# Attention, second half: the key low parts as full-array products in even column tiles, from a zero-padded copy of the queries' high parts

## The chip, the cores and the metric

The kernel runs on one core of one Trainium2 chip. The metric is device time in microseconds (us): before the change 2640.49 us, the median of three runs (2640.45 to 2641.33). The profile and the trace are of one further execution, taken by the hardware profiler.

## The reference, cut to what matters

One layer of a hybrid encoder: a projection of 2048 tokens (a grid of 32 rows by 64 columns) feeds a gated linear recurrence and a 2-D neighbourhood attention with 16 heads of 64 dimensions. Both results go through one output projection. The change touches the scores of the attention alone.

```python
h = layernorm(x) * (1 + scale) + shift
proj = h @ w_in                                   # (2048, 9216)
q_h, i_h, zf_fw, zf_bw, g_h, q_n, k_n, v_n, g_n = split(proj)
y_hg = hgrn2_branch(q_h, i_h, zf_fw, zf_bw, g_h, ...)
# attention: a query at (row, col) sees a window of 8 rows x 16 columns
s = einsum('bhjqd,bhrjcd->bhjqrc', q_row, k_blk) * 64 ** -0.5
s = where(col_mask, s + bias, -inf)
o = einsum('bhjqrc,bhrjcd->bhjqd', softmax(s), v_blk)
y = concat([y_hg, o * silu(g_n)]) @ w_out
x = layernorm(alpha * x + gate * y) * ln_g + ln_b
```

## The kernel before, in words

The stages in time, in us of the profiled execution: the start (to 15), the first half of the attention (to 520), the recurrence (to 1757), the second half of the attention (to about 2320), and the rest of the output projection and the last norm (to 2639). The 16 heads are eight pairs in each half; a pair's two heads lie on partitions 0 to 63 and 64 to 127.

Products are made nearly exact with a split into a high and a low part of a shorter float type. The dense projections (L278) are three products: high x high, high x low, low x high. In the scores the same is done in two steps. Each head has a tile `Q` of 128 rows, its 64 high rows and its 64 low rows, and `KA` (for one head) or `KB` (for the other) holds the high part of the keys twice, so one product over 128 rows (L1015) gives (high + low) q x high k. The second product (L1018) adds high q x low k, with `KL` holding both heads' low parts on their halves of the partitions: 64 rows for each head, so the two heads' products use the two halves of the array.

In the second half a pair has three row blocks R = 1, 2, 3 and in each four column tiles j = 0 to 3; a tile has 128 queries per head and 360 (j = 0, 3) or 480 (j = 1, 2) keys for R = 1 and 2, and 288 or 384 for R = 3. The *even* tiles are j = 0 and 2. A tile's chain: scores on TensorE (PE) into two banks; `shifted` on VectorE (DVE, L1027) adds the bias and finds the extreme; `powers` on ScalarE (ACT, L1032) takes the exponential and its sum; `shares` on DVE (L1036, L1037) divides; `turned` transposes on PE (L1060) and copies the result to `pt`, the first head on DVE (L1064), the second on ACT (L1066); `sums` multiplies by V on PE (L1082, 64 columns of the array per head). After four tiles the output is gated on DVE into `yv` (L1092) and written to `yq` (L1093).

`natten_woven` sets PE's order by hand: scores of tile i; behind an odd tile the sums of two tiles; a piece of dense work for the next pair (L278, in the first pair also the V projection L291, in the last the output projection L1448 to L1450); the transposes of tile i−1; dense work again; then the preparation of later tiles (`st.k` L952 to L954, `st.q` L936 to L939, `st.gate` L970, `st.v` L963). So an even tile's scores are followed on PE by dense work, an odd tile's by sums. ACT, DVE, POOL and SP (which issues the DMAs) are put in order by a scheduler that estimates when things are ready; `tc.high_priority` moves work ahead in it. Weights come from DRAM to `wr`, ACT copies the high part `wh` (L778), DVE takes the rest `wl` (L779). The output projection's weights are loaded by `wo_load` and split by `wo_split` (L1408, L1409) in the last pairs. L297 copies a bank of the V projection to `vt`.

The `pbuf` tiles hold the scores from `shifted` to `turned`, used in turn; there are five in this half.

```python
if i % 2 and len(pipe) > 2:
    for _ in range(2):
        m, r, c, pts = pipe.pop(0)
        m.sums(r, c, pts)
yield 1
turn(pipe, 2)
yield 1
```

Of the kernel before, what the change touches and what calls it, by code (L numbers as in the profile page):

```python
# [10 lines left out]
F32 = mybir.dt.float32  # L11
F32R = mybir.dt.float32r
U32 = mybir.dt.uint32
AF = mybir.ActivationFunctionType
# [5 lines left out]
P = 128  # L20
# [10 lines left out]
PRI = 1500  # L31
# [7 lines left out]
def body(ctx: ExitStack, tc: tile.TileContext, t):  # L39
    nc = tc.nc  # L40
    dve, act, pool, pe = nc.vector, nc.scalar, nc.gpsimd, nc.tensor
# [85 lines left out]
    def pinned(ins):  # L127
        return tc.keep_in_program_order(ins)
# [604 lines left out]
    pbuf, pb_i = [], [0]  # L733

    def natten_init(n, half):
        pbuf.clear()
        cur["bias"] = (11, 15)[half]
        for i in range(n):
            b = tl("pbuf")
            pool.memset(b[:, 264:512], 0.0)  # L740
            pbuf.append(b)
        keysets.clear()
        for i in range(2 - half):
            keysets.append({z: tl(f"{z}{i}", F32R, [P, (12, 28)[half] * GW]) for z in ("KA", "KB", "KL")})

    NCOL = (("q", 5120), ("k", 6144), ("g", 8192))
    NCOL0 = (("k", 6144), ("q", 5120), ("g", 8192))
# [162 lines left out]
    keysets = []  # L910
# [82 lines left out]
    class Natten:  # L993
# [8 lines left out]
        def scores(self, R, j):  # L1002
            k0, nr = TILE[R]
            bt = self.st.table(KIND[R], j)
            kw = KW[j]
            nk, b0 = nr * kw, KC[j] - KS[j]
            scs = [ps("sc"), ps("sc")]
            qs = [z[:, j * P:(j + 1) * P] for z in self.st.Q[R]]
            keys = keysets[self.p % len(keysets)]

            def kv(z):
                return keys[z].rearrange("p (r c) -> p r c", c=GW)[:, k0 - self.r_base:k0 - self.r_base + nr, KC[j]:KC[j] + kw]

            for hh in range(2):
                pe.matmul(scs[hh][:, 0:nk], qs[hh], kv(("KA", "KB")[hh]), start=True, stop=False, skip_group_check=True)  # L1015
            for hh in range(2):
                hs_ = slice(hh * 64, hh * 64 + 64)
                pe.matmul(scs[hh][:, 0:nk], qs[hh][hs_], kv("KL")[hs_], start=False, stop=True, skip_group_check=True)  # L1018
            out, mxs = [], []

            def shifted(hh):
                s, sc = pbuf[pb_i[0] % len(pbuf)], scs[hh]
                pb_i[0] += 1
                mx = cp.tile([P, 3], F32, tag="mx", name=nm("mx"), bufs=6)
                out.append(s)
                mxs.append(mx)
                return dve.tensor_tensor_reduce(s[:, 0:nk].rearrange("p (r c) -> p r c", c=kw), sc[:, 0:nk].rearrange("p (r c) -> p r c", c=kw),  # L1027
                                                bt[:, 0:nr, hh, b0:b0 + kw], scale=-0.125, scalar=3.0e38, op0=ALU.add, op1=ALU.min, accum_out=mx[:, 0:1])

            def powers(hh):  # L1030
                s, mx = out[hh], mxs[hh]
                act.activation(s[:, 0:nk], s[:, 0:nk], AF.Exp, scale=-1.0, bias=mx[:, 0:1], accum_out=mx[:, 1:2])  # L1032

            def shares(hh):
                s, mx = out[hh], mxs[hh]
                dve.reciprocal(mx[:, 2:3], mx[:, 1:2])  # L1036
                dve.tensor_scalar(s[:, 0:nk], s[:, 0:nk], mx[:, 2:3], 1.0, op0=ALU.mult, op1=ALU.mult)  # L1037

            with tc.high_priority(offset=PRI):
                if self.half:  # L1040
                    for hh in range(2):
                        shifted(hh)
                        powers(hh)
                        shares(hh)
                else:
                    for hh in range(2):
                        pinned(shifted(hh))
                    for f in (powers, shares):
                        for hh in range(2):
                            f(hh)  # L1050
            return out
# [56 lines left out]
    def natten_woven(st, nxt, pipe, extra=None, finish=False):  # L1108

        n = Natten(st)  # L1110
        if st.half:
            now, later = prep_now(st), prep_next(nxt) if nxt else {}
        else:
            now, later = {0: [(st.table, "top", 3)]}, first_next(nxt) if nxt else {}
        extra = extra or {}
        for i, (R, j) in enumerate(n.order):
            pipe.append([n, R, j, n.scores(R, j)])
            if i % 2 and len(pipe) > 2:
                for _ in range(2):
                    m, r, c, pts = pipe.pop(0)  # L1120
# [4 lines that stand above are left out]
            for f, *a in now.get(i, []) + later.get(i, []) + extra.get(i, []):  # L1125
                f(*a)
        if finish:
# [3 lines that stand above are left out]
            turn(pipe, 1)  # L1131
# [13 lines left out]
    HB = {"c": 3, "qi0": 1, "qi1": 2, "v": 2, "pm": 1, "ub": 1, "Sf": 5, "Sb": 5, "pd": 1, "dec": 4, "decb": 1, "dsuf": 1, "g": 3, "ei": 1, "de": 2, "ke": 1, "kx": 1, "qx": 1, "x": 4, "t": 2, "cl": 3, "rh": 1, "rl": 1}  # L1145
    SB_ = {"ada": 4, "x": 16, "nb": 1}
    NB0 = {"V": 6, "pbuf": 4, "pt": 4, "yv": 1, "bias": 3, "x": 8, "s": 3}
    NB1 = {"V": 6, "pbuf": 5, "pt": 4, "yv": 1, "bias": 3, "Q": 6}
    SMS = {"raw": "e", "s": "sg", "w0": "bk", "w1": "q", "w2": "vt", "w2l": "gt", "vo": "vt"}
    SM0 = {"raw": "e", "Q": "q", "sg": "sg", "e": "e", "q": "q", "vo": "vt", "gt": "gt"}  # L1150
    SMH = {"V0": "gt", "e": "e", "q": "q", "vo": "vt", "gt": "gt", "sg": "sg", "raw": "e", "bk": "bk"}
    SM1 = {"raw": "e", "sg": "sg", "vo": "vt", "bk": "bk", "V2": "q", "wr": "vt", "wr2": "gt"}

    def startup():

# [203 lines left out]
    with psum_phase("n0", NPS), tc.manual_schedule(engines={mybir.EngineType.PE}):  # L1359
        with phase("st", SB_, SMS), tc.manual_schedule(engines={getattr(mybir.EngineType, e) for e in ("PE", "SP", "Activation", "DVE")}):  # L1360
            raws, feed = startup()
        with phase("n0", NB0, SM0):
            natten_init(4, 0)
            st = first_half(raws, feed)
# [146 lines left out]
    LU = 6  # L1511
    LP = 0
    with psum_phase("n1", NPS), phase("n1", NB1, SM1), tc.manual_schedule(engines={mybir.EngineType.PE}):
        natten_init(5, 1)
        st = st0
        for f, *a in ((st.k, 0), (st.k, 1), (st.k, 2), (st.q, 1), (st.table, "mid", 0), (st.table, "mid", 1), (st.v, 2), (st.v, 3), (st.table, "mid", 3), (st.q, 2), (st.v, 4), (st.gate, 1)):
            f(*a)
        vs = vstream(2, 3)
        for _ in range(5):
# [5 lines left out]
        for u in range(8):  # L1525
            nxt, extra = None, None
            if u < 7:
# [4 lines left out]
                nxt = Prep(u + 1, 1, raws)  # L1532
# [8 lines left out]
            st = nxt  # L1541
# [77 lines left out]
```

## Time and profile before

| | us |
|---|---|
| median of three runs | 2640.49 |
| lowest and highest | 2640.45, 2641.33 |
| the profiled execution's own time | 2641.48 |
| its span in the trace | 2639.3 |
| PE busy | 2574.2 (98%) |
| weight loads (PEld) busy | 2140.4 (81%) |
| DVE busy | 1738.7 (66%) |
| ACT busy | 1402.7 (53%) |
| POOL busy | 106.4 (4%) |

Lines such as L1018 are lines of the kernel before. A row of the timeline is the start, the duration of the whole row in us, the engine, line, operation, output and inputs, the tile used of the array (128*128, or 64*128 for half of its rows), the shape and the number of instructions put together in the row; behind it in brackets the idle time of the engine just before and what ended it. PE's matmuls are pipelined, so the distance of two starts says more than a duration. PEld is the load of weights into the array. A row of waits is the line that waits, what it waits for, the total, the number and the longest; "issue" stands where the trace shows nothing that the engine waited for.

### The profile page before, as it was taken

The page shows a single profiled execution, that of the slowest core. Times are in us where ns is not written, and L with a number is a line of the kernel's source. Part 1 is how long each engine was busy: PE and PEld are TensorE (multiplying, and loading weights), DVE is VectorE, ACT ScalarE, POOL GpSimd, SP SyncE. Part 2 cuts the span into 40 slices and gives each one's busy share as a digit, 9 for nine tenths or more (in the row PEclk, how much of TensorE's full clock was granted, in tenths as well). Part 3 has the DMA queues.
Part 4 walks back from the last instruction along what each step waited for, and adds up shares of the span by engine and source line. Part 5 has one row for each costly group of instructions (what it writes and reads, how often), then busy time and mean ns, then how long its engine had stood idle before and what let it go on. Part 6 is the DMA issues. An engine that isn't in the chain of part 4 may idle for free.

```text
span 2639.3 us, 45745 instructions
## 1 busy us (share of the span) xinstructions
PE 2574.2 (98%) x17140; PEld 2140.4 (81%) x17140; DVE 1738.7 (66%) x4354; ACT 1402.7 (53%) x2808; POOL 106.4 (4%) x142
## 2 busy tenths in 40 slices
PE   6999999989999999999999999999999999999998
PEld 5888888878888888888888888888777777788887
DVE  7444545477777778877787777555777778548443
ACT  4534445366666666666666666454666667431110
POOL 0000000000000000000000000000000000042221
PEclk9999999999999999999999999999999999999999
DMA  7465454212121126212221222345454455443331
GB/s 271 140 212 142 127 169 155 95 49 69 65 65 57 65 73 219 85 46 76 76 65 57 73 72 75 109 129 157 125 137 137 140 142 162 117 155 128 96 96 56
DMA packets 225629, 295.86 MB, mean 112 GB/s; under 512 B 28807, under 2 KB 117511, under 8 KB 224263
## 3 DMA queue, kind: packets, MB, share of 16 engines
q1 hardware_dynamic: 225407, 292.93, 36.3%
q8 instruction: 135, 2.21, 0.4%
q14 instruction: 87, 0.71, 0.1%
HBM read 217.65 MB, written 66.99 MB: 108 GB/s over the span
## 4 chain that ended last, share of the span: by engine, by line
PE 74%; ACT 2%; DVE 1%; DMA 1%; issue 0%; DVEq 0%; ACTq 0%
PE pj L278 40%; PE ps L1448 4%; PE ps L1450 4%; PE ps L1449 4%; PE ps L1082 3%; PE ps L1060 3%; PE pj L291 3%; PE ps L478 2%; PE ps L470 1%; PE ps L1018 1%; PE ps L1015 1%; PE ps L545 1%; PE ps L569 1%; PE ps L517 1%; PE ps L571 1%; DMA yq<-t 1%
## 5 line engine op out<-in xcount | busy, mean ns | idle before, releaser
L278 PE MATMUL pj<-h,wh 128*128 128x512 f32 x4000 | 1277.8, 400 | 4.2 <-ACT wh L803 1.9
L278 PEld LDWEIGHTS pj<-h,wh 128*128 128x128 f32 x4000 | 722.9, 188 | 163.0 <-issue 20.3
L278 PE MATMUL pj<-h,wl 128*128 128x512 f32 x2000 | 784.0, 392 | 0.0
L278 PEld LDWEIGHTS pj<-h,wl 128*128 128x128 f32 x2000 | 375.7, 188 | 83.3 <-DVE wl L779 0.4
L1032 ACT ACTIVATE pbuf<-pbuf,mx 128x480 f32<-128x480 f32 (+5 forms) x256 | 152.7, 598 | 150.1 <-DVE mx L1027 149.5
L1027 DVE CUSTOM_DVE_ANT_1 pbuf<-ps,bias 128x480 f32<-128x480 f32 (+5 forms) x256 | 129.4, 540 | 120.4 <-PE ps L1018 105.5
L291 PE MATMUL pj<-wh,h 128*128 128x256 f32 x1024 | 197.8, 288 | 2.8 <-ACT vt L297 2.5
L291 PEld LDWEIGHTS pj<-wh,h 128*128 128x128 f32 x1024 | 164.5, 193 | 7.2 <-ACT vt L297 3.2
L268 ACT ACTIVATE wh<-wr 128x512 fp32r<-128x512 f32 x192 | 120.3, 627 | 80.9 <-PE pj L278 71.8
L269 DVE TENSOR_TENSOR wl<-wr,wh 128x512 fp32r<-128x512 f32 x192 | 131.5, 685 | 45.2 <-ACT wh L268 43.7
L291 PE MATMUL pj<-wl,h 128*128 128x256 f32 x512 | 145.4, 284 | 0.0
L1066 ACT ACTIVATE pt<-ps 120x384 f32<-120x384 f32 (+3 forms) x128 | 65.3, 511 | 127.3 <-PE ps L1060 126.9
L464 DVE TENSOR_TENSOR de<-e,de 128x512 f32<-128x512 f32 x64 | 44.3, 692 | 118.0 <-ACT de L463 118.0
L1064 DVE COPY pt<-ps 120x384 f32<-120x384 f32 (+3 forms) x128 | 75.0, 586 | 68.1 <-PE ps L1060 67.4
L1060 PE MATMUL ps<-ident,pbuf 128*128 128x128 f32 (+2 forms) x832 | 112.3, 273 | 0.7 <-DVE pbuf L1037 0.7
L1060 PEld LDWEIGHTS ps<-ident,pbuf 128*128 128x128 f32 (+2 forms) x832 | 97.5, 137 | 17.1 <-ACT pbuf L1032 1.1
L752 ACT ACTIVATE e<-pj 128x512 f32<-128x512 f32 x98 | 58.4, 596 | 87.2 <-PE pj L278 80.4
L1037 DVE TENSOR_SCALAR pbuf<-pbuf,mx 128x480 f32<-128x480 f32 (+5 forms) x256 | 101.4, 408 | 4.4
L1424 ACT ACTIVATE yh<-yr 128x512 fp32r<-128x512 f32 x52 | 32.7, 629 | 131.8 <-PE ps L1449 113.5
L1497 DVE TENSOR_TENSOR vt<-ps,gt 128x512 f32<-128x512 f32 x24 | 16.5, 692 | 128.9 <-PE ps L1450 128.9
L291 PEld LDWEIGHTS pj<-wl,h 128*128 128x128 f32 x512 | 98.8, 193 | 1.5 <-issue 0.5
L445 DVE TENSOR_TENSOR_SCAN c<-c,g 128x128 f32<-128x128 f32 x256 | 88.3, 403 | 10.7 <-ACT c L435 10.7
(268 smaller groups left out, 4642.5 us busy)
## 6 DMA issues: line engine op xcount, KB each, us to landing
wr<-in_w_in SPq DMA_DIRECT2D x276, 256.0 KB
yr<-yq SPq DMA_DIRECT2D x64, 256.0 KB
bias<-tint SPq DMA_DIRECT2D x24, 480.0 KB
x<-in_x SPq DMA_DIRECT2D x32, 256.0 KB
ada<-in_ada_m SPq DMA_DIRECT2D x8, 1024.0 KB
wr<-in_w_v SPq DMA_DIRECT2D x32, 256.0 KB
nv<-vt SPq DMA_DIRECT2D x32, 256.0 KB
yq<-yv SPq DMA_DIRECT2D x32, 256.0 KB
```

The lines of the kernel that those rows point to most:

```text
L268: act.activation(hi, raw, AF.Copy)
L269: dve.tensor_tensor(lo, raw, hi, op=ALU.subtract)
L278: pe.matmul(pz, a, b, start=(k == 0 and n == 0), stop=(k == KT - 1 and n == 2))
L291: pe.matmul(pzs[tp][:, i * 256:(i + 1) * 256], a, b, start=(k == 0 and n == 0 and i == 0), stop=(k == KT - 1 and n == 2), skip_group_check ...
L445: dve.tensor_tensor_scan(c[:, sl], c[:, sl], L[:, sl], 0.0, op0=ALU.add, op1=ALU.subtract)
L1027: return dve.tensor_tensor_reduce(s[:, 0:nk].rearrange("p (r c) -> p r c", c=kw), sc[:, 0:nk].rearrange("p (r c) -> p r c", c=kw), bt[:, 0 ...
L1032: act.activation(s[:, 0:nk], s[:, 0:nk], AF.Exp, scale=-1.0, bias=mx[:, 0:1], accum_out=mx[:, 1:2])
L1037: dve.tensor_scalar(s[:, 0:nk], s[:, 0:nk], mx[:, 2:3], 1.0, op0=ALU.mult, op1=ALU.mult)
L1060: pe.transpose(ptp[0:cw, c * P:(c + 1) * P], s[:, c * cw:(c + 1) * cw], ident)
L1448: pe.matmul(pz, yh[:, kk], wh, start=first, stop=False)
L1449: pe.matmul(pz, yh[:, kk], wl, start=False, stop=False)
L1450: pe.matmul(pz, yl[:, kk], wh, start=False, stop=last)
```

## The change

In the second half a new tile `Z` of 128 rows and 2 x 512 columns (4 KB per partition) holds the high part of the queries of one row block: the first 512 columns have the first head's on rows 0 to 63 and zeros below, the second 512 the second head's on rows 64 to 127 and zeros above. POOL writes the zeros once. `alone` copies the two high parts into it on ACT, with high priority: once at the start of the half, and then behind the scores of each tile j = 2 for the next row block, or for the next pair's first one, 24 times in all. In even tiles the low product of each head is now one product over all 128 rows, `Z`'s columns against `KL`; odd tiles keep the 64-row form. To find the space, there are four `pbuf` tiles in place of five, and `yv` has no buffer of its own but takes one of the four of the tag `vt`, which the V projection's outputs and the loaded w_out weights use as well.

```diff
@@ natten_init
+        if half:
+            keysets[0]["Z"] = tl("Z", F32R, [P, 2 * 512])
+            pool.memset(keysets[0]["Z"][64:128, 0:512].bitcast(F32), 0.0)
+            pool.memset(keysets[0]["Z"][0:64, 512:1024].bitcast(F32), 0.0)
+    def alone(st, R):
+        z = keysets[0]["Z"]
+        with tc.high_priority(offset=PRI):
+            for hh in range(2):
+                hs_ = slice(hh * 64, hh * 64 + 64)
+                act.activation(z[hs_, hh * 512:(hh + 1) * 512], st.Q[R][hh][hs_], AF.Copy)
@@ scores
             for hh in range(2):
                 hs_ = slice(hh * 64, hh * 64 + 64)
-                pe.matmul(scs[hh][:, 0:nk], qs[hh][hs_], kv("KL")[hs_], start=False, stop=True, skip_group_check=True)
+                if self.half and j % 2 == 0:
+                    o = hh * 512 + j * P
+                    pe.matmul(scs[hh][:, 0:nk], keys["Z"][:, o:o + P], kv("KL"), start=False, stop=True, skip_group_check=True)
+                else:
+                    pe.matmul(scs[hh][:, 0:nk], qs[hh][hs_], kv("KL")[hs_], start=False, stop=True, skip_group_check=True)
@@ natten_woven
             pipe.append([n, R, j, n.scores(R, j)])
+            if st.half and j == 2 and (R < 3 or nxt):
+                alone(*((st, R + 1) if R < 3 else (nxt, 1)))
@@ buffers of the second half
-    NB1 = {"V": 6, "pbuf": 5, "pt": 4, "yv": 1, "bias": 3, "Q": 6}
+    NB1 = {"V": 6, "pbuf": 4, "pt": 4, "bias": 3, "Q": 6}
-    SM1 = {"raw": "e", "sg": "sg", "vo": "vt", "bk": "bk", "V2": "q", "wr": "vt", "wr2": "gt"}
+    SM1 = {"raw": "e", "sg": "sg", "vo": "vt", "yv": "vt", "bk": "bk", "V2": "q", "wr": "vt", "wr2": "gt"}
@@ start of the second half
-        natten_init(5, 1)
+        natten_init(4, 1)
-        for f, *a in (..., (st.q, 1), (st.table, "mid", 0), ...):
+        for f, *a in (..., (st.q, 1), (alone, st, 1), (st.table, "mid", 0), ...):
```

On PE no instruction changes its place. The orders of ACT and DVE do change; lines move by 12 to 16 in the changed kernel (L297 stays, the exponential L1032 is L1048, L1027 is L1043, L1037 is L1053, the copies into Z are L756). The first place is ACT at the start of the second half, before: `Q` is the high part of the queries, `sg` a gate, `vt` the V projection's output.

```order
L937 ACTIVATE Q_19061<-e_18010 64x512
L970 ACTIVATE sg_19066<-e_18260 128x512
L970 ACTIVATE sg_19348<-e_18304 128x512
L297 ACTIVATE vt_18842<-pj_18744 128x512
L297 ACTIVATE vt_18845<-pj_18745 128x512
L338 ACTIVATE sg_18714<-sg_18714 128x512
```

And the same place of the changed kernel.

```order
L949 ACTIVATE Q_19064<-e_18010 64x512
L982 ACTIVATE sg_19069<-e_18260 128x512
L982 ACTIVATE sg_19353<-e_18304 128x512
L756 ACTIVATE Z_18661<-Q_18682 64x512
L756 ACTIVATE Z_18661<-Q_18683 64x512
L297 ACTIVATE vt_18845<-pj_18747 128x512
L297 ACTIVATE vt_18848<-pj_18748 128x512
L338 ACTIVATE sg_18717<-sg_18717 128x512
```

The two copies stand ahead of the L297 that empties the V projection's banks.

The second place is ACT at tile (R = 3, j = 2) of pair 3, before: the exponentials of the two heads (`pbuf`), two weight splits (`wh`), the second head's transposed copy (`pt`), the next keys (`KA`).

```order
L752 ACTIVATE e_22140<-pj_22015 128x512
L1032 ACTIVATE pbuf_18652,mx_22152<-pbuf_18652,mx_22152 128x384
L1032 ACTIVATE pbuf_18654,mx_22157<-pbuf_18654,mx_22157 128x384
L778 ACTIVATE wh_22168<-wr_22011 128x512
L778 ACTIVATE wh_22172<-wr_22013 128x512
L1066 ACTIVATE pt_22186<-ps_22182 128x384
L952 ACTIVATE KA_3548_18660<-e_21874 64x256
```

And in the changed kernel.

```order
L764 ACTIVATE e_22165<-pj_22040 128x512
L756 ACTIVATE Z_18661<-Q_21834 64x512
L756 ACTIVATE Z_18661<-Q_21835 64x512
L790 ACTIVATE wh_22195<-wr_22036 128x512
L790 ACTIVATE wh_22199<-wr_22038 128x512
L1048 ACTIVATE pbuf_18650,mx_22177<-pbuf_18650,mx_22177 128x384
L1048 ACTIVATE pbuf_18652,mx_22182<-pbuf_18652,mx_22182 128x384
L1082 ACTIVATE pt_22213<-ps_22209 128x384
L964 ACTIVATE KA_3547_18658<-e_21897 64x256
```

Both copies and both splits now stand ahead of the exponentials; on DVE the splits' remainders (L779, now L791) accordingly stand ahead of the two shares.

The third place is DVE one tile later, before: reciprocals, shares (TENSOR_SCALAR) of tile (R = 3, j = 3) of width 288, and the shift (ISA) of the next pair's first tile, 360 wide.

```order
L1036 RECIPROCAL mx_22212<-mx_22212 128x1
L1064 COPY pt_22245<-ps_22241 128x384
L1036 RECIPROCAL mx_22217<-mx_22217 128x1
L1037 TENSOR_SCALAR pbuf_18656<-pbuf_18656,mx_22212 128x288
L1027 ISA pbuf_18650,mx_22272<-ps_22266,bias_22081 128x360
L1027 ISA mx_22272 128x1
L1037 TENSOR_SCALAR pbuf_18658<-pbuf_18658,mx_22217 128x288
L1027 ISA pbuf_18652,mx_22277<-ps_22267,bias_22081 128x360
L1027 ISA mx_22277 128x1
```

And in the changed kernel.

```order
L1052 RECIPROCAL mx_22239<-mx_22239 128x1
L1080 COPY pt_22272<-ps_22268 128x384
L1052 RECIPROCAL mx_22244<-mx_22244 128x1
L1053 TENSOR_SCALAR pbuf_18654<-pbuf_18654,mx_22239 128x288
L1043 ISA pbuf_18650,mx_22299<-ps_22293,bias_22106 128x360
L1043 ISA mx_22299 128x1
L1043 ISA pbuf_18652,mx_22304<-ps_22294,bias_22106 128x360
L1043 ISA mx_22304 128x1
L1053 TENSOR_SCALAR pbuf_18656<-pbuf_18656,mx_22244 128x288
```

The second head's share, which its transposes on PE read, now stands behind both shifts of the next pair's first tile.

More of the change, by code (lines that the diff above doesn't have):

```diff
@@ L1513, in body @@
     with psum_phase("n1", NPS), phase("n1", NB1, SM1), tc.manual_schedule(engines={mybir.EngineType.PE}):
-        natten_init(5, 1)
+        natten_init(4, 1)
         st = st0
-        for f, *a in ((st.k, 0), (st.k, 1), (st.k, 2), (st.q, 1), (st.table, "mid", 0), (st.table, "mid", 1), (st.v, 2), (st.v, 3), (st.table, "mid", 3), (st.q, 2), (st.v, 4), (st.gate, 1)):
+        for f, *a in ((st.k, 0), (st.k, 1), (st.k, 2), (st.q, 1), (alone, st, 1), (st.table, "mid", 0), (st.table, "mid", 1), (st.v, 2), (st.v, 3), (st.table, "mid", 3), (st.q, 2), (st.v, 4), (st.gate, 1)):
             f(*a)
```

## The prediction

> **What bounds the kernel now.** I read the page first, then busy time by stretch, the waits of TensorE and of its weight loads in the second half, and last the timeline of single tiles. The first fence holds the page's row of engines and the row of busy time over pairs 1 to 5 of the second half (stretch and length in us, then busy us and instructions of PE, PEld, DVE, ACT and POOL, then the TensorE clock, DMA share and GB/s).
>
> ```profile
> PE 2574.2 (98%) x17140; PEld 2140.4 (81%) x17140; DVE 1738.7 (66%) x4354; ACT 1402.7 (53%) x2808; POOL 106.4 (4%) x142
> 1858.00:2237.00 379.00, 378.32 (x2597) 298.23 (x2596) 295.97 (x896) 251.33 (x592) 5.49 (x18) 1.00 0.50 140
> ```
>
> PE is busy 378.3 of 379 us at full clock: there TensorE is the bound and nearly any time taken from its stream comes off the end. DVE (296) and ACT (251) have room on average, but what counts is where one wait ends last. The next rows are waits between 1700 and 2330 us (waiting line, what it waits for, us in total, times, longest).
>
> ```profile
> PE pj L1448 <- ACT yh L1440: 7.3, 2, 6.1
> PE pj L291 <- ACT vt L297: 2.5, 1, 2.5
> PE ps L1060 <- DVE pbuf L1037: 0.7, 1, 0.7
> PEld ps L1018 <- issue: 25.0, 96, 0.4
> ```
>
> Matmuls wait for other engines in few places, and I come back to three. The last row is where the change bites: all 96 tiles show the weight load of the half-array product (L1018) held up with nothing visible to wait for, 0.26 us each. What that costs on PE is seen in one even tile of 360 keys (start, duration, engine, line).
>
> ```profile
> 2006.27 0.32 PE L1015 MATMUL ps<-KA,Q 128*128 128x360 f32 x1
> 2006.43 0.33 PE L1015 MATMUL ps<-KB,Q 128*128 128x360 f32 x1
> 2006.69 0.43 PE L1018 MATMUL ps<-KL,Q 64*128 64x360 f32 x2
> 2007.05 0.73 PE L278 MATMUL pj<-h,wh 128*128 128x512 f32 x2
> 2007.62 0.40 PE L278 MATMUL pj<-h,wl 128*128 128x512 f32 x1
> 2007.86 0.62 PE L278 MATMUL pj<-h,wh 128*128 128x512 f32 x2
> 2008.32 0.40 PE L278 MATMUL pj<-h,wl 128*128 128x512 f32 x1
> ```
>
> Full-array products follow each other by 0.16 us (KA to KB), and projections by 0.23 (2007.62 to 2008.32 is three steps). But KB to the half-array pair takes 0.26, and the pair to the first projection 0.36, although the pair streams its 360 columns side by side (two matmuls in one row, 0.43 from the first start to the last end). The first two projections then take 0.57 where 0.46 would do. A tile of 480 keys shows the same.
>
> ```profile
> 2016.78 0.38 PE L1015 MATMUL ps<-KA,Q 128*128 128x480 f32 x1
> 2017.00 0.38 PE L1015 MATMUL ps<-KB,Q 128*128 128x480 f32 x1
> 2017.31 0.49 PE L1018 MATMUL ps<-KL,Q 64*128 64x480 f32 x2
> 2017.73 0.73 PE L278 MATMUL pj<-h,wh 128*128 128x512 f32 x2
> 2018.31 0.39 PE L278 MATMUL pj<-h,wl 128*128 128x512 f32 x1
> ```
>
> I read this as the array emptying when its row split changes, once going into the half-array form and once coming out.
>
> **The change part by part.** *The even tile.* In the new form the two low products are full-array with the same width as KA and KB, so I expect KA, KB, Z, Z, projection in even steps. With 360 keys the way from KB to the third projection now is 2007.62 − 2006.43 = 1.19; then three steps of 0.16 and two of 0.23 make 0.94: a gain of 0.25. With 480 keys it is 1.31 against 3 × 0.22 + 0.46 = 1.12: a gain of 0.19, since the added stream is longer. The six even tiles of a pair are 2 × 360, 2 × 480, 384 and 288 wide, mean 392; on the line through both points that is 0.234, and 48 tiles give **−11.2 us**. Odd tiles keep the old form.
>
> The Trainium skill, *TensorEngine Tiling (Array Packing)*, under Key Properties, says that a change of tiling mode drains the TensorE. The trace agrees as far as it shows 0.26 and 0.36 us where neighbours take 0.16 and 0.23.
>
> *What it adds.* 24 times two ACT copies of 64x512 (same form as L937 below, 0.65 a piece with its step), 31 us of ACT in 560. Two memsets on POOL are hidden: POOL is 4% busy, and they need only the space of the phase before. Four pbuf instead of five cost nothing: tile i+2 takes the buffers of tile i, whose transposes stand ahead of its scores on PE. Now the places where the copies stand ahead of somebody.
>
> *Start of the half.* The rows are ACT's queue, the PE wait, and the clock (after length and PE busy, the granted share, then DMA share and GB/s).
>
> ```profile
> 1758.04 0.63 ACT L937 ACTIVATE Q<-e 64x512 fp32r<-64x512 f32 x1
> 1758.69 1.15 ACT L970 ACTIVATE sg<-e 128x512 f32<-128x512 f32 x2
> 1759.74 1.07 ACT L297 ACTIVATE vt<-pj 128x512 f32<-128x512 f32 x2
> 1760.37 0.38 PE L291 MATMUL pj<-wh,h 128*128 128x256 f32 x1 [2.49 <-ACT vt L297]
> 1761.00:1762.00 1.00, 1.00 (x9) 0.87 0.51 112
> 1762.00:1763.00 1.00, 1.00 (x6) 0.50 0.53 143
> 1765.00:1766.00 1.00, 1.00 (x7) 0.92 0.28 83
> ```
>
> ACT goes from one to the next without a gap, and PE stands 2.49 us until L297 empties its bank. The two copies now stand ahead of L297, behind the L970s: 2 × 0.65 = **+1.3 us**, all on the path. The stall is already followed by a stretch at half clock: a share of 0.87 puts its start 0.26 us before 1762 and one of 0.92 its end 0.16 after 1765, 3.4 us in all, which cost PE half of that, 1.7. I put nothing more on it; a second such stretch, another 1.7, is the upper end, and nothing beyond 1.3 saved or lost is the lower.
>
> The Trainium skill, *TensorE: Matmul & The Clock Gate*, Part 1, describes a clock gate that judges activity in windows of some 3.4 us. By it a longer idle could spoil one more window, and the sum would be about −4.8 in place of −6.5; the low stretch here fits one window, and no run here yet shows two.
>
> *(R3, j2) in pairs 1 to 5.* Here the copies and two weight splits go ahead of both exponentials, so the chain behind them is late. Pair 3:
>
> ```profile
> 2038.87 0.56 DVE L1027 CUSTOM_DVE_ANT_1 pbuf<-ps,bias 128x384 f32<-128x384 f32 x1 [1.89 <-PE ps L1018]
> 2039.47 0.62 ACT L1032 ACTIVATE pbuf<-pbuf,mx 128x384 f32<-128x384 f32 x1 [1.41 <-DVE mx L1027]
> 2040.69 1.14 ACT L778 ACTIVATE wh<-wr 128x512 fp32r<-128x512 f32 x2
> 2041.73 0.47 ACT L1066 ACTIVATE pt<-ps 128x384 f32<-128x384 f32 x1
> 2042.63 0.94 ACT L952 ACTIVATE KA<-e 64x256 fp32r<-64x256 f32 x2 [0.43 <-PE ps L1015]
> 2043.18 0.46 DVE L1027 CUSTOM_DVE_ANT_1 pbuf<-ps,bias 128x288 f32<-128x288 f32 x1 [0.22 <-issue]
> 2048.80 0.37 DVE L1037 TENSOR_SCALAR pbuf<-pbuf,mx 128x288 f32<-128x288 f32 x1
> 2049.08 0.53 DVE L1027 CUSTOM_DVE_ANT_1 pbuf<-ps,bias 128x360 f32<-128x360 f32 x1
> 2049.55 0.82 PE L1060 MATMUL ps<-ident,pbuf 128*96 128x128 f32 x6
> ```
>
> ACT idles 1.41 us there, but the copies may only start when the product is done, at about 2038.9, where DVE starts. Then 1.3 of copies, 1.1 of splits and 1.2 of exponentials (2039.47 to 2040.69) end at 2042.5, and the shares on DVE, 0.4 each and some 0.1 for the reciprocals, at 2043.4. So L1027 of the next tile begins there at about 2043.5 in place of 2043.18, 0.3 to 0.5 later with its reading, and DVE then runs almost without a break to the L1037 at 2048.80. That share, the second head's, now ends at 2049.17; in the new order it stands behind the second L1027 of the tile after (2049.08), another 0.45 later. Its head's transposes are the second three of the row at 2049.55, needed from 2049.85 on; that leaves 0.7 today. With 0.3 + 0.45 of delay, and PE arriving up to 0.46 earlier through two even tiles just before, PE would wait 0.5: **+2.5 us** in five pairs (0.5 to 4.0, by 0.1 to 0.8 a pair).
>
> *The other j2 tiles* have the copies in the same gap, with more room behind. (R2, j2) of pair 3:
>
> ```profile
> 2021.14 0.58 ACT L1066 ACTIVATE pt<-ps 128x512 f32<-128x512 f32 x1
> 2022.96 0.83 PE L1082 MATMUL ps<-pt,V 128*64 128x128 f32 x12
> ```
>
> The copy L1066 ends at 2021.72 and its product starts 1.2 us later. Since 0.68 of the 1.3 fits into ACT's wait for DVE, I put 0.6 on L1066 and 0.2 on PE's side; it still holds with some 0.4 to spare. I take 0, at most 0.2 in each of 16 places.
>
> *Pair 6* has the weight work of the output projection as well.
>
> ```profile
> 2207.43 0.70 ACT L1032 ACTIVATE pbuf<-pbuf,mx 128x480 f32<-128x480 f32 x1 [0.68 <-DVE mx L1027]
> 2219.40 0.84 PE L1060 MATMUL ps<-ident,pbuf 128*120 128x128 f32 x6 [0.68 <-DVE pbuf L1037]
> ```
>
> From the first row to 2217 ACT has hardly a gap, and at the second PE already stands 0.68. Of the copies' 1.3, 0.68 fits into the wait of the first row; the other 0.6 is handed through ACT and DVE to the transposes, and what the tile in front gains there is lost to the wait: **+0.7 us** (0.4 to 1.5).
>
> *Pair 7.* The 6.1-us wait of L1448 is set by ACT's yh, not by PE's own pace, so the gain of the tile inside it is void: **+0.2**.
>
> *The shared buffers.* The first four w_out loads now come out of the tag that yv uses too, so the last of them waits, on SP's queue with the V loads behind it, until the yq write of pair 6's first yv.
>
> ```profile
> 2203.65 0.41 SPq L1093 DMA_DIRECT2D yq<-yv  x1
> 2213.78 1.15 ACT L1408 ACTIVATE wo<-vt 128x512 fp32r<-128x512 f32 x2
> ```
>
> From that write's issue to the split that needs the last load are 10 us, for a write and a read of 256 KB: 0, at most 1.
>
> **Sum:** −11.2 + 1.3 + 2.5 + 0.7 + 0.2 = **−6.5 us**. On the profiled execution's 2641.48 that makes 2635.0. That execution is 0.99 over the median of the three runs, with the same stages, so the forecast against the median is 2640.49 − 6.5 = **2634.0**.
>
> **The rivals.** *A, the forecast* (chance 0.55): 2634.0, give or take 1.8 for the terms' bounds.
>
> *B, all copies hidden but those at the start* (0.16). Gaps such as the 1.41 above take up the rest, and only the start's 1.3 remains: −11.2 + 1.3 = −9.9, 2630.6. For it: one wait for L1037 in the whole half today. Against it: the 0.7 us at (R3, j3), less than the delays that I count there.
>
> *C, the copies cost at nearly all 24 places* (0.2). They have priority and stand ahead of exponentials and of L1066, and a faster PE meets them sooner. At 0.3 us in each of the 18 places beside the start and (R3, j2) of pairs 1 to 5: −11.2 + 1.3 + 2.5 + 5.4 = −2.0, 2638.5. From 0.41 a place on the gain is gone. For it: ACT at 66% in these pairs (251 of 379), and slack of 0.4 to 0.7 in the tiles above. Against it: most copies fall into a wait for DVE.
>
> *D, the other side: the delay is not the switch of form* (0.09). If the 0.26 and 0.36 belonged to the low product as such (its operands, its load), they would stay, and the full-array form only adds: two products that ran side by side now go one behind the other. That is one more stream per tile, 0.16 at 360 and 0.22 at 480, 0.18 at the mean: +8.6 in 48 tiles, with the 1.3 + 2.5 + 0.7 above +13.1, 2653.6. It decides as soon as less than 0.18 of the tile's 0.41 beyond even steps (0.234 + 0.18) is due to the switch. Against it: KA to KB uses operands of the same kind at the same clock and takes 0.16, and the delay sits on both sides of the pair, also on the projections that share nothing with it. For it: no row shows this product in another form. The Trainium skill, *TensorEngine Tiling (Array Packing)*, Theoretical Speedup, gives row tiling up to 2x where the contraction is 64 or less; by that rule alone undoing it is a loss, and the pair in one row shows that the side-by-side part is real.
>
> **How the numbers follow.** The point is A's 2634.0. About 0.2% (5.3 us) is what a measurement of this kernel can tell from no change: faster is below 2635.2, slower above 2645.8. A lies below 2635.2 for three quarters of its 0.55, B wholly, C for a little: 0.60. The rest of A and C with the small part of D near no change is 0.32; D gives 0.08. The range goes from B's 2630.6 to C's 2638.5, each with what the two-digit rows leave open in the gain (0.01 a tile, 0.5): 2630.1 to 2639.0. It leaves out D, and the outer part of C.
>
> **What would show it.** In the profile after: the weight-load wait on the half-array line falls from 96 to 48 times, and the new low products have none; KB to Z to Z to the projection goes in steps of 0.16 at 360 keys. The wait of L291 at the start grows from 2.5 to 3.8. Waits of transposes for the shares, one now, become five of about 0.5 and one of about 1.2; the wait of L1448 grows by about 0.2. PE's busy time should fall by about 11. I am wrong if Z's steps show 0.26 or more (D), if waits of L1060 or L1082 sum to over 8 us (C), or if a second half-clock stretch follows the start.

## The result: 5.5 us faster, and the profile after

The changed kernel takes 2635.17 us (median of 13 runs, 2630.94 to 2636.96), the kernel before in runs beside it 2640.64 (13 runs). The ratio is 0.998, with a 95% interval of 0.9971 to 0.9988: faster by 0.2%, or 3 to 8 us. The forecast was 2634.0 in a range of 2630.1 to 2639.0. The profiled execution took 2634.39 us, with a span of 2632.5 against 2639.3.

First the page's row of engines and the busy time over pairs 1 to 5, as for the kernel before.

```profile
PE 2564.7 (97%) x17140; PEld 2150.0 (82%) x17140; DVE 1736.9 (66%) x4354; ACT 1430.8 (54%) x2856; POOL 108.7 (4%) x143
1858.00:2237.00 379.00, 372.07 (x2599) 305.21 (x2597) 299.77 (x912) 278.17 (x642) 6.79 (x18) 1.00 0.53 144
```

PE is busy 9.5 us less on the page, where some 11 were forecast; ACT 28 us more: the copies. PE's 372.1 of 379 us isn't a new idleness: everything comes some 6 us earlier, and so most of the 6.2-us wait of pair 7, which ends at 2237.93 in place of 2243.83, now falls into the end of this stretch. Here are the waits of PE and of its weight loads, 1700 to 2330 us (L1466 is the old L1448, L1076 the old L1060, L1034 the half-array product).

```profile
PE pj L1466 <- ACT yh L1458: 7.4, 2, 6.2
PE pj L291 <- ACT vt L297: 3.8, 1, 3.8
PE ps L1076 <- DVE pbuf L1053: 1.3, 1, 1.3
PEld ps L1034 <- issue: 12.4, 48, 0.3
PEld ps L1076 <- DVE pbuf L1053: 1.6, 5, 0.3
```

The unexplained waits of the half-array's weight load fell from 96 to 48 times and from 25.0 to 12.4 us, and the new line L1032 has none. The five waits of transposes that the forecast announced are there too, on the weight load of L1076 and with 0.3 each. The same tiles of 360 and 480 keys as before, now with the full-array low product (L1032):

```profile
2003.70 0.32 PE L1027 MATMUL ps<-KA,Q 128*128 128x360 f32 x1
2003.87 0.33 PE L1027 MATMUL ps<-KB,Q 128*128 128x360 f32 x1
2004.03 0.49 PE L1032 MATMUL ps<-KL,Z 128*128 128x360 f32 x2
2004.36 0.63 PE L278 MATMUL pj<-h,wh 128*128 128x512 f32 x2
2004.83 0.39 PE L278 MATMUL pj<-h,wl 128*128 128x512 f32 x1
...
2014.18 0.38 PE L1027 MATMUL ps<-KB,Q 128*128 128x480 f32 x1
2014.40 0.61 PE L1032 MATMUL ps<-KL,Z 128*128 128x480 f32 x2
2014.85 0.63 PE L278 MATMUL pj<-h,wh 128*128 128x512 f32 x2
2015.31 0.39 PE L278 MATMUL pj<-h,wl 128*128 128x512 f32 x1
```

KB to Z takes 0.16 us, the two Z to the projection 0.33, and the first two projections 0.47: KB to the third projection is 0.96 in place of 1.19. At 480 keys it is 1.13 in place of 1.31.

KA, KB, Z, Z and the projection now go in even steps of one stream, against rival D. To see where the rest went, I compare the start of each tile (its first matmul, the KA product) with that of the same tile in the kernel before. The level just ahead of the half differs from run to run, so it is taken off: in this execution the last V projection before the wait ends at 1756.93 in place of 1757.88, 0.95 early for reasons that lie before the change. All numbers are us against the kernel before, minus is earlier. "Start" is the first tile less that level, "boundary" what the first tile of pairs 2 to 6 adds (the middle one of five; an undisturbed even tile of 360 keys adds −0.23), "pair 6" what (R3, j0) adds there (undisturbed −0.26), "half" the last tile less the level. A row is one execution, so "half" isn't the gain of the median beside it; the medians of the kernel before, measured beside each run, were 2640.64 (changed), 2640.30 (changed_again), 2639.65 (also_j1 and the three runs whose names begin with copies) and 2639.68 (the others).

| kernel | wait L291 | start | boundary | pair 6 | half | median of all its runs |
|---|---|---|---|---|---|---|
| changed | 3.8 | +2.33 | +0.04 | +0.38 | −6.13 | 2635.17 |
| changed_again | 3.8 | +1.54 | +0.06 | +0.37 | −5.83 | 2635.52 |
| copies_only | 3.8 | +1.25 | 0.00 | +3.78 | +5.85 | 2646.73 |
| also_j1 | 3.8 | +1.57 | +0.05 | +0.37 | −5.10 | 2636.52 |
| copies_pool | 2.5 | +0.20 | −0.23 | +0.51 | −9.32 | 2632.84 |
| copies_dve | 2.5 | +0.06 | −0.03 | +3.01 | +4.55 | 2639.60 |
| buffers_only | 2.5 | +0.26 | 0.00 | 0.00 | −0.67 | 2640.47 |
| half_z_act | 3.4 | −0.35 | −0.23 | +0.37 | −9.93 | 2632.99 |
| half_z_pool | 2.5 | +0.25 | −0.23 | +0.16 | −10.99 | 2629.72 |

In the changed kernel the other even tiles of pairs 1 to 5 add −0.16 to −0.26, the odd ones 0.00 to 0.02. The column "start" needs one correction. The kernel before runs the first 0.6 us of its first tile still at half clock (that tile starts at 1764.57, the low clock ends at about 1765.16), and where the low clock is over by then the first tile is 0.27 to 0.29 us shorter, in buffers_only as well, which has none of the change's products. Read at the second tile, with the 0.23 of the first even tile given back where there is one, the start is +2.06 (changed), +1.32 (changed_again), +1.28 (copies_only) and +1.30 (also_j1); it is 0.0 to −0.2 in the four runs with a wait of 2.5 us, and −0.6 in half_z_act. So the trace's −6.13 is a gain of 10.3 in the tiles (1.31 in the even ones of a pair, less 0.02 in the odd ones, times eight) less 2.06 at the start, less five times 0.27 at the boundaries, less 0.64 in pair 6 and 0.15 in pair 7.

Three places in rows. At the start (ACT, PE, and the clock in the windows where it sinks and rises):

```profile
1758.79 1.26 ACT L756 ACTIVATE Z<-Q 64x512 fp32r<-64x512 f32 x2
1760.07 1.08 ACT L297 ACTIVATE vt<-pj 128x512 f32<-128x512 f32 x2
1760.72 0.58 PE L291 MATMUL pj<-wh,h 128*128 128x256 f32 x1 [3.79 <-ACT vt L297]
1759.00:1760.00 1.00, 0.00 (x0) 0.52 0.51 148
1765.00:1766.00 1.00, 1.00 (x7) 0.57 0.22 69
```

The two copies put 1.30 on the wait (3.79 against 2.49). Beside that the clock stays at half from about 1759.0 to 1765.9, 6.8 us in place of 3.4. The first 1.7 us of this fall into the wait itself, where PE has nothing to do; it works 5.1 us at half clock in place of 3.4, so by half of the difference this costs 0.9 more.

At a pair boundary, (R3, j3) of pair 3 (DVE's shift of that tile, the second head's share, and the transposes):

```profile
2039.96 0.45 DVE L1043 CUSTOM_DVE_ANT_1 pbuf<-ps,bias 128x288 f32<-128x288 f32 x1
2046.03 0.36 DVE L1053 TENSOR_SCALAR pbuf<-pbuf,mx 128x288 f32<-128x288 f32 x1
2045.89 1.10 PE L1076 MATMUL ps<-ident,pbuf 128*96 128x128 f32 x6
```

The six transposes take 1.10 in place of 0.82 us: the last three wait 0.28 for the share that ends at 2046.39. And in pair 6 (ACT's second split of w_out, then the transposes on PE):

```profile
2206.79 0.64 ACT L1426 ACTIVATE wo<-vt 128x512 fp32r<-128x512 f32 x1 [0.18 <-DMA vt<-in_w_out]
2213.73 0.84 PE L1076 MATMUL ps<-ident,pbuf 128*120 128x128 f32 x6 [1.30 <-DVE pbuf L1053]
```

### The profile page after: what moved, and what is told of

Same layout as the page of the kernel before. It is cut to its first block, busy times and chain, and to the rows that moved or that the text cites. A ratio compares the mean times of both kernels' runs of the same rounds, so it can differ in the third digit from the quotient of the medians.

```text
span 2632.5 us, 45805 instructions
## 1 busy us (share of the span) xinstructions
PE 2564.7 (97%) x17140; PEld 2150.0 (82%) x17140; DVE 1736.9 (66%) x4354; ACT 1430.8 (54%) x2856; POOL 108.7 (4%) x143
## 4 chain that ended last, share of the span: by engine, by line
PE 73%; DVE 3%; ACT 2%; DMA 1%; issue 0%; DVEq 0%; ACTq 0%
PE pj L278 39%; PE ps L1466 4%; PE ps L1467 4%; PE ps L1468 4%; PE pj L291 3%; PE ps L1098 3%; PE ps L1076 2%; PE ps L478 2%; PE ps L470 1%; PE ps L545 1%; PE ps L1027 1%; PE ps L569 1%; PE ps L517 1%; PE ps L571 1%; PE ps L643 1%; DMA yq<-t 1%
## 5 line engine op out<-in xcount | busy, mean ns | idle before, releaser
L1048 ACT ACTIVATE pbuf<-pbuf,mx 128x480 f32<-128x480 f32 (+5 forms) x256 | 152.4, 597 | 114.0 <-DVE mx L1043 113.2
L291 PE MATMUL pj<-wh,h 128*128 128x256 f32 x1024 | 198.8, 289 | 4.1 <-ACT vt L297 3.8
L1043 DVE CUSTOM_DVE_ANT_1 pbuf<-ps,bias 128x480 f32<-128x480 f32 (+5 forms) x256 | 129.1, 540 | 105.1 <-PE ps L1034 47.1
L291 PEld LDWEIGHTS pj<-wh,h 128*128 128x128 f32 x1024 | 165.5, 194 | 7.9 <-ACT vt L297 4.5
L291 PE MATMUL pj<-wl,h 128*128 128x256 f32 x512 | 146.1, 285 | 0.0
L1076 PE MATMUL ps<-ident,pbuf 128*128 128x128 f32 (+2 forms) x832 | 113.3, 274 | 1.7 <-DVE pbuf L1053 1.3
L1076 PEld LDWEIGHTS ps<-ident,pbuf 128*128 128x128 f32 (+2 forms) x832 | 97.2, 137 | 19.3 <-ACT pbuf L1048 1.7
L1053 DVE TENSOR_SCALAR pbuf<-pbuf,mx 128x480 f32<-128x480 f32 (+5 forms) x256 | 101.2, 413 | 3.9
L291 PEld LDWEIGHTS pj<-wl,h 128*128 128x128 f32 x512 | 99.5, 194 | 1.4 <-issue 0.5
```

The lines of the kernel that those rows point to most:

```text
L291: pe.matmul(pzs[tp][:, i * 256:(i + 1) * 256], a, b, start=(k == 0 and n == 0 and i == 0), stop=(k == KT - 1 and n == 2), skip_group_check ...
L1076: pe.transpose(ptp[0:cw, c * P:(c + 1) * P], s[:, c * cw:(c + 1) * cw], ident)
```

## Experiments

The theory: each even tile gains because the array no longer changes its form around the low product; the copies themselves are hidden and cost only where they, or the order that they bring with them, stand ahead of somebody. The rivals: the copies cost everywhere (and the even tile's gain is larger); the half-array product is slow as such; the shared buffers cost.

**copies_only.** The copies are made and the buffers changed, but the low products are the old ones.

```diff
-                if self.half and j % 2 == 0:
+                if False:
```

> Everything of the change but its use: Z is filled 24 times and the buffers are the changed ones, but all low products keep the 64-row form. By the forecast's theory (the gain is the switch of the array's form in even tiles, and the copies cost only where they stand ahead of somebody) KB to L1034 keeps 0.26 us in even tiles and no gain is left; the start costs 1.3 us of wait and up to 1 us more of low clock, pair 6 costs 0.4 to 0.6, the pair boundaries nothing, since DVE's order here has the second share ahead of both shifts: 2 to 3 us slower than the kernel before. By the rival that copies cost at nearly every place (0.3 us each) it is 7 to 9 us slower.

Measured: ratio 1.0029 (1.0018 to 1.0040), some 7 us slower, over what the theory expected and about what the rival did. The tile starts tell which it is. From the first tile to (R3, j0) of pair 6 they stay at +1.25 to +1.28: the 18 places with copies in pairs 0 to 5 add 0.00 us, so the rival that copies cost everywhere is out. All the rest falls in at pair 6 and behind it (+3.78, then +0.8). ACT, PE's waits, and on SP's queue the write of yv and the load:

```profile
2212.67 0.63 ACT L1426 ACTIVATE wo<-vt 128x512 fp32r<-128x512 f32 x1
2217.19 0.63 ACT L1426 ACTIVATE wo<-vt 128x512 fp32r<-128x512 f32 x1 [3.90 <-DMA vt<-in_w_out]
PE ps L1076 <- DVE pbuf L1053: 3.1, 2, 2.9
2207.55 0.91 SPq L1109 DMA_DIRECT2D yq<-vt  x1
2213.53 0.34 SPq L1421 DMA_DIRECT2D vt<-in_w_out  x1
```

The fourth load of w_out, issued at 2213.53, holds ACT for 3.9 us. It waits for a buffer that yv had, as the forecast said, but the split that needs it is the second one and not the one at 2213.78 that the forecast looked at. The load leaves SP's queue 6.0 us behind the write of yv here and 5.8 in the changed kernel, and in both the queue's last wait before it is for that write to land (1.6 and 2.5 us). So the two loads of keys that stand ahead of it here, and behind it in the changed kernel, aren't what delays it. What differs is the write: it leaves 5.1 us ahead of ACT's first split here, 8.4 us in the changed kernel (2197.56 and 2205.98), and so the load costs ACT 3.9 us here and 0.18 there. Just ahead of this late write a load of V took 2.9 us to issue, for which the trace shows no cause.

**buffers_only.** The changed buffers without copies.

```diff
-            if st.half and j == 2 and (R < 3 or nxt):
-                alone(*((st, R + 1) if R < 3 else (nxt, 1)))
-        for f, *a in (..., (st.q, 1), (alone, st, 1), ...):
+        for f, *a in (..., (st.q, 1), ...):
-                if self.half and j % 2 == 0:
+                if False:
```

> The kernel before with the changed buffers alone (Z set aside and zeroed but never filled or used, four pbuf, yv in the tag vt). By what the runs so far suggest, four pbuf cost nothing, the start and pairs 0 to 5 stay within 0.1 us, and the shared tag costs in pair 6: ACT's second split of w_out waits for its DMA for 0 to 4 us, and PE up to as much, so 0 to 5 us slower than the kernel before, all of it after (R3, j0) of pair 6. If the shared tag is harmless (the forecast's term of 0 to 1 us), no tile start differs by more than 0.3 us from the kernel before.

Measured: ratio 1.0004 (0.9995 to 1.0013). Tile starts stay within 0.01 us from the second tile to the end of pair 6; ACT's wait for the second w_out split is 0.6 us and reaches nobody; only pair 7 comes 0.6 us earlier. So four pbuf and the shared tag cost PE nothing in this execution. They aren't without effect, though: DVE's shift of (R1, j1), always 1.06 us behind its tile's start on PE in the kernel before, comes 2.2 us later in pair 2, where the trace names a bias table as what it waits for, and 1.6 in pair 3. Every run with four pbuf shows such a late shift in some of the pairs, the two without the shared tag too.

**also_j1.** The full-array form in tiles j = 1 too, in front of the 64-column sums.

```diff
-                if self.half and j % 2 == 0:
+                if self.half and j < 3:
```

> The changed kernel, with the full-array form in tiles j = 1 as well, which are followed by the sums in the 64-column form, so that a switch remains behind them. If the switch is what delays, 24 tiles of 480 or 384 keys save 0.09 us on the way in, add a stream of 0.18 to 0.22 and keep the way out: 2 to 3 us slower than the changed kernel, and Z to L1098 keeps some 0.4 us. If the half-array product as such were slow, each such tile would gain about 0.2 us as the even ones did: 4 to 5 us faster than the changed kernel.

Measured: 2636.52, ratio 0.9988 (0.9979 to 0.9998). Neither number came: in pairs 1 to 6 a tile j = 1 adds −0.03 to 0.03 us, not +0.1 and not −0.2. (The −5.10 in the table holds 1.5 us lost at (R1, j2) of pairs 4 and 6, each time right behind a late bias table.) First the tile (R2, j1) of pair 3 in the kernel before, then in this one:

```profile
2010.82 0.39 PE L1015 MATMUL ps<-KB,Q 128*128 128x480 f32 x1
2011.14 0.49 PE L1018 MATMUL ps<-KL,Q 64*128 64x480 f32 x2
2011.56 1.21 PE L1082 MATMUL ps<-pt,V 128*64 128x128 f32 x18
```

```profile
2007.29 0.38 PE L1027 MATMUL ps<-KB,Q 128*128 128x480 f32 x1
2007.51 0.61 PE L1032 MATMUL ps<-KL,Z 128*128 128x480 f32 x2
2008.05 0.98 PE L1098 MATMUL ps<-pt,V 128*64 128x128 f32 x14
```

Before, 0.10 over a stream of 0.22 on the way in, and 0.42 from the pair to the sums, 0.20 over its stream. Now no delay on the way in, two streams (0.44), and 0.10 over them into the sums. So, in these rows, leaving the half-array form costs 0.20 in front of both followers, and entering the half-row form or the half-column form from the full array costs 0.10 each. One switch fewer saves 0.2 here, the added stream takes 0.22. The product as such isn't slow, or this tile would have gained 0.2: this too speaks against rival D. My expectation was wrong in leaving the way out at 0.4.

**copies_pool.** The copies on POOL.

```diff
-                act.activation(z[hs_, hh * 512:(hh + 1) * 512], st.Q[R][hh][hs_], AF.Copy)
+                pool.tensor_scalar(z[hs_, hh * 512:(hh + 1) * 512], st.Q[R][hh][hs_], 1.0, None, op0=ALU.mult)
```

> The changed kernel with the copies into Z made by POOL, which is idle there, as multiplications by one. By the forecast's theory the even tiles keep their gain (about 10.5 us) and the three costs go: the wait of L291 is 2.5 us again, the second share at the pair boundaries stands between the two shifts as in the kernel before, so that those waits go from 0.28 us to under 0.1, and the wait in pair 6 is 0.7 us plus its lost gain: 3 to 4 us faster than the changed kernel, 9 to 10 faster than before. Rival: POOL's copies slow DVE's reads and writes or come too late for the next tile j = 0, and waits of L1032 or of the shares eat what ACT gave back.

Measured: 2632.84, ratio 0.9976 (0.9966 to 0.9986); half −9.32, 3.2 better than the changed kernel. Waits of PE, and POOL's group of copies (busy us, mean ns of one, idle before):

```profile
PE pj L291 <- ACT vt L297: 2.5, 1, 2.5
PE ps L1076 <- DVE pbuf L1053: 1.4, 1, 1.4
L756 POOL TENSOR_SCALAR Z<-Q 64x512 fp32r<-64x512 f32 x48 | 77.1, 1606 | 379.0 <-PE ps L1032 345.9 <-ACT Q L948 31.2
```

A copy takes 1.6 us there against 0.63 on ACT, and no wait of PE shows for it. The medians differ by 6.8 us, under the expected 9 to 10. The start is back at 2.5, and the boundary steps are whole (−0.23): DVE's order has the share between the two shifts again.

**copies_dve.** The copies on DVE.

```diff
-                act.activation(z[hs_, hh * 512:(hh + 1) * 512], st.Q[R][hh][hs_], AF.Copy)
+                dve.tensor_copy(z[hs_, hh * 512:(hh + 1) * 512], st.Q[R][hh][hs_])
```

> The changed kernel with the copies into Z made by DVE. ACT's order is as in the kernel before, so the wait of L291 at the start is 2.5 us again. At the pair boundaries DVE's order still has the second share behind both shifts: if that order is the cause of the 0.28 us there, the waits stay or grow by some 0.2 us; if ACT's copies were the cause they go. In all 0 to 2 us faster than the changed kernel.

Measured: ratio 1.0002 (0.9993 to 1.0012), and the profiled execution was the slowest of its ten. The boundary step is −0.03, a wait of 0.2, with ACT's queue as before and the share behind both shifts: the order is enough for it. What I missed is elsewhere, PE's waits for shares and DVE's for the bias tables:

```profile
PE ps L1076 <- DVE pbuf L1053: 6.1, 5, 2.4
DVE pbuf L1043 <- DMA bias<-tint: 22.1, 5, 5.6
```

DVE waits 22 us for bias tables, which the kernel before shows nowhere, and pairs 2 to 6 then lose about 1 to 3 us each in tiles that were whole in pair 1. The changed kernel has the same wait at 4.5 us, still covered, and buffers_only at 3.8, so it doesn't come from the copies alone; also_j1 has it at 12.8. In the kernel before the last load of a table (L722) leaves SP's queue 2.4 to 4.3 us ahead of tile (R1, j1) in pairs 2 to 6, in this run 0.1 to 2.6. Why it leaves later was not tried. This execution is 7.1 us over the median of its kernel, so most executions can't lose as much in all.

**half_z_act, half_z_pool.** Z holds only the column tiles that are used, j = 0 and 2: 2 KB instead of 4, copies of 64x256, and yv has its own buffer again (the memsets and the tags follow). In half_z_pool the same two copies go to POOL.

```diff
-            keysets[0]["Z"] = tl("Z", F32R, [P, 2 * 512])
+            keysets[0]["Z"] = tl("Z", F32R, [P, 2 * 256])
-                act.activation(z[hs_, hh * 512:(hh + 1) * 512], st.Q[R][hh][hs_], AF.Copy)
+                act.activation(z[hs_, hh * 256:(hh + 1) * 256].rearrange("p (k c) -> p k c", c=P), st.Q[R][hh][hs_].rearrange("p (k t c) -> p k t c", t=2, c=P)[:, :, 0], AF.Copy)
-                    o = hh * 512 + j * P
+                    o = hh * 256 + j // 2 * P
-    NB1 = {..., "pbuf": 4, "pt": 4, "bias": 3, "Q": 6}
+    NB1 = {..., "pbuf": 4, "pt": 4, "yv": 1, "bias": 3, "Q": 6}
```

> The changed kernel with Z of only the two column tiles that are used: 2 KB in place of 4, copies of 64x256 by ACT, and yv has its own buffer again, so that the w_out loads are where they were in the kernel before. Even tiles gain the same 10.4 us. Start: two copies of about 0.43 us, so the wait of L291 grows to 3.3. Pair boundaries: DVE's order here has the second share ahead of both shifts, so no wait there if the order is the cause (0.28 us each if it is ACT's copies). Pair 6: no wait for the w_out DMA; under 0.5 us lost. Together 2 to 3 us faster than the changed kernel, 7.5 to 9 faster than before.

> As the one before, with the copies by POOL. The wait of L291 is 2.5 us, no wait at the pair boundaries, and pair 6 keeps only the 0.7 us of the kernel before plus the gain lost in it (0.2): about 9.5 us faster than the kernel before at the last tile. If pair 6's loss in the changed kernel came from the copies and not from the shared tag, this one gains nothing there over the run with full-size copies on POOL (which lost 0.5 at that place).

Measured: 2632.99, ratio 0.9975 (0.9965 to 0.9985), and 2629.72, ratio 0.9966 (0.9954 to 0.9978). Waits of PE in half_z_act, then in half_z_pool:

```profile
PE pj L291 <- ACT vt L297: 3.4, 1, 3.4
PE ps L1076 <- DVE pbuf L1053: 1.3, 1, 1.3
```

```profile
PE pj L291 <- ACT vt L297: 2.5, 1, 2.5
PE ps L1076 <- DVE pbuf L1053: 1.1, 1, 1.1
```

With half the copy the boundary is whole on ACT as well (−0.23), the share standing ahead of both shifts there. Pair 6 still loses 0.63 with short copies on ACT and without the shared tag, and 0.42 with them on POOL. The 0.42 is as much as the two even tiles just ahead of the wait gain (0.17 and 0.26), so I read it as gain that the older wait swallows, and the other 0.2 as ACT's queue. On POOL, full size with the shared tag, it is 0.77, where ACT waits 1.2 us for w_out. By its median half_z_pool is the fastest version, 10 us under the kernel before; its interval overlaps those of half_z_act and copies_pool. Its −10.99 holds 1.1 us from the first tile of pair 7, behind the wait for ACT's yh.

**changed_again.** The changed kernel once more.

> The changed kernel once more, nothing altered. What is open is the start of the half: in its profile the low clock lasted 6.8 us there, in that of the run with unused copies, which has the same wait of 3.8 us, 3.2 us. If two low stretches belong to this wait, they come again and the first tile is late by 2.2 to 2.4 us over the state before the wait; if it is a matter of where the wait falls, the wait is 3.8 us again, the low clock lasts some other time (0, 3.4 or 6.8 us) and the first tile is late by 0 to 2.4. The other steps (tiles, pair boundaries 0.28 us, pair 6) repeat within 0.1 us.

Measured: 2635.52, ratio 0.9978 (0.9968 to 0.9988). The wait is 3.8 again; the clock, a new wait of PE, and in pair 6 the bias table's load and DVE's shift of (R1, j1):

```profile
1763.00:1764.00 1.00, 1.00 (x8) 0.72 0.35 110
1766.00:1767.00 1.00, 1.00 (x7) 0.58 0.28 82
PE ps L1076 <- DVE mx L1052: 1.6, 1, 1.6
2173.02 0.64 SPq L722 DMA_DIRECT2D bias<-tint  x1
2177.50 0.66 DVE L1043 CUSTOM_DVE_ANT_1 pbuf<-ps,bias 128x480 f32<-128x480 f32 x1 [4.07 <-PE ps L1076]
```

The low clock lasts from about 1763.4 to 1766.8, one stretch of 3.4 us and not two, and the start costs 1.54, or 1.32 at the second tile. So the length of the wait doesn't decide: with the same 3.8 us the low clock began 2.1 us behind the wait's start in the first trace and 4.9 here, a wait of 2.5 us was followed by 3.4 us of it in five kernels, and half_z_act, with 3.36 us of wait, had none at all there and a start even 0.35 better than before. The wait of 1.6 us is in pair 6. The table's load left SP's queue at 2173.02, 2168.07 in the first trace, and the shift stood 4.07 us where it stood 0.68; PE lost 1.8 us there. The trace names PE's transposes for the 4.07, but PE began the scores of that tile only 1.0 us later than in the first trace, so a late table, as in also_j1 and copies_dve, is the likelier cause. It isn't shown.

## Why the prediction was right

The time fell within the range, and the main mechanism held. That the sum came within 0.4 us in the profiled execution is partly luck: three terms were off by 0.8 to 1.1 and made up for each other. One of the forecast's own signs of being wrong, a second half-clock stretch behind the start, did come in that execution and not in the second.

**The even tile.** Right in mechanism, shown by Z's even steps and by also_j1. The size was 10.3 us, 0.9 under the 11.2: two rows gave 0.25 and 0.19 where the steps are 0.23 to 0.25 and 0.17 to 0.19, and odd tiles lose 0.02 a pair. The drain that the Trainium skill, *TensorEngine Tiling (Array Packing)*, names under Key Properties is 0.10 us into the half-row form and 0.20 out of it plus 0.1 at the next product; the side-by-side gain under Theoretical Speedup is there as well (one stream of 0.16 to 0.22 saved), and is smaller than the switches.

**The start.** The wait's growth was 1.30, as forecast. The term was 1.3; read at the second tile it measured 2.06 in the profiled execution and 1.32, 1.28 and 1.30 in the three other runs with full copies on ACT. So the term itself was right, and what it left out is the second low stretch: 6.8 us at half clock in that execution, 3.4 in the others. It cost 0.8 and not the 1.7 of the forecast's upper end, since 1.7 us of it fell into the wait. A low stretch that comes once or twice behind the same wait is the case that the Trainium skill, *TensorE: Matmul & The Clock Gate*, Part 1, describes: windows of about 3.4 us that don't care where the work falls. Both traces agree with it, 3.4 and 6.8 us: the low clock lasts one window or two.

**(R3, j2).** Forecast 0.5 a pair, measured 0.27 to 0.28 in each of five pairs, 1.4 in place of 2.5. The step that failed is DVE's 0.3 us of delay at the next shift: it began at 2039.96, 3.22 earlier, as much as PE's scores of (R3, j2) (3.23), since DVE did the splits' remainders while it would have waited for ACT, and its old gap of 0.22 ahead of the shift is gone. The other half, the share behind both shifts (0.45), was right, and three runs show that this order makes the wait: copies_dve keeps the order without copies on ACT and loses 0.2, half_z_act keeps copies on ACT without the order and loses nothing, nor does copies_pool.

**The other j2 tiles.** Forecast 0, measured 0.00 in copies_only and no lost gain in the changed kernel. **Pair 6** 0.7, measured 0.64, but not of the parts that I added: with copies 0.4 us shorter in all half_z_act loses the same 0.63, and half_z_pool with none on ACT still 0.42, so most of it is gain lost ahead of the old wait and at most some 0.2 the copies on ACT, for which I had 0.6. **Pair 7** 0.2, measured 0.15; that is luck as well, as its first tile adds −1.35 to +0.03 in the other runs with Z in use. **The shared buffers** 0 to 1, measured 0.18 us on ACT and none of it shown on PE; right by luck, since the split that waits was another than the one I checked, with no 10 us to spare, and copies_only paid 3.8 us there. That four pbuf cost nothing held for PE in the profiled execution; the later bias tables I hadn't seen.

**The sum.** −6.5 forecast; −6.1 and −5.8 in the two traces at the last tile, −5.5 in the medians. In the first a smaller gain (0.9) and a dearer start (0.8) were largely paid by the cheaper boundaries (1.1); in the second the start came as forecast, and the delay in pair 6 took its place.

## What to carry to other kernels

Two half-array products side by side save one stream, but the two changes of form around them cost about 0.4 us if full-array work stands on both sides; as long as a stream takes less than that (0.16 to 0.22 us here), pad with zeros and run them one behind the other. Check which part of an operand is used before copying all of it, and put such copies on an engine that is idle: the copies themselves cost nothing in most places, their position ahead of somebody did. When a buffer is shared to make room, look at which transfer now has to wait for it, and at the first instruction that needs that transfer.

## What the runs showed that I had not expected

A wait of the same 3.8 us was followed by 6.8 us at half clock in one execution and by 3.4 in three, and one of 3.4 us by none. Entering the half-row or the half-column form costs the same 0.10 us from the full array, while leaving the half-row form costs 0.20 into either. With one pbuf less, bias tables came late to DVE in some pairs of every run; in most this cost PE nothing, in one execution up to 3 us a pair. The copy of 64x512 that takes ACT 0.63 us takes POOL 1.6.
